# Block exchange on POOL's queue, later readers, the residual put away to DRAM, and probabilities of five head groups turned on VectorE and by DMA

## The chip, the core and the metric

The kernel runs on one core of a Trainium2 chip. The metric is the device time of one execution in microseconds, the median of several runs. TensorE (PE) multiplies, ScalarE (ACT) and VectorE (DVE) prepare and finish tiles, GpSimd (POOL) does small work and issues DMAs, SyncE (SP) issues DMAs.

## What is computed

Two transformer blocks on one sequence of 256 tokens of width 2048, in float32. The first has forget-gate ("fox") attention with 16 heads of 128 and a feed-forward part with a causal convolution of width 3; the second has 8 heads of dilated attention beside gated linear attention (GLA), and a SiLU-gated feed-forward part. Cut to the shape of the work:

```
h  = x
h += fox_attention(rms(h) @ w1) @ w2          # 16 heads, 4 groups of 4
h += (silu(conv(gate)) * conv(val)) @ w4      # gate, val = split(rms(h) @ w3), 2 x 5632 columns
q, k, v, ... = split(rms(h) @ w5)
h += concat(gla(...), dilated_attention(...)) @ w6   # 8 dilated heads, 2 groups of 4
h += (silu(rms(h) @ w7g) * (rms(h) @ w7u)) @ w8
```

The softmax of one head is `p = softmax(q k^T * scale + bias)`, causal, and its output `p v`.

## The kernel before

**Weights.** `plan` lists every weight tile, 128 x 2048, in order of use. `dma_to` loads them from SP's queue into three `raw` buffers. `split_to` turns half a tile at a time into a high part `wh` (a cast on ScalarE, line 105) and a low part `wl` (a subtraction on VectorE, line 111), five buffers of each. `gemm` walks over column blocks of 512 and, within one, over units: a unit is half a weight tile, and `mm3` (lines 118 to 120) makes twelve products of 128 x 512 of it. Before unit u is multiplied, the split of unit u + 4 is recorded (`LEAD = 4`), so ScalarE and VectorE may come up to four units late before TensorE stands still.

**Order.** Nothing reorders the program: every engine runs its instructions as they are recorded. All work beside the weight products is in generators. `gemm` calls `pump` after each unit but the last of a block, and `pump` takes one step of every generator in `fast` and of the first in `slow` (two steps of the latter while `rate[0]` is 2). After the last unit it starts the block's `evac` instead. A `yield` is therefore the distance of one unit, and a value is waited for by the engine whose next instruction reads it.

**Block exchange.** A block of 256 tokens x 512 columns has to be turned before it can be multiplied again. `flip` turns 32x32 pieces on VectorE (line 296), writes them in four DMAs, the legs, to a DRAM tile `way` (line 300) and reads it back in one, the return (line 304), all from SP's queue. Steps: transpose, one yield, legs, one yield, return, two yields, then the reader (`ordered`, line 316, four ScalarE operations that put the pieces in order into a new tile, or `split_flipped`). There are 54 flips, 216 legs.

**Attention.** For each group of four heads `plain` scales q and k, `head_norm` norms them (the square on ScalarE, the sum on VectorE, root and multiplication on POOL), `flip` turns them, and `box["kf"]` opens the generator `attention`: `s2` for scores and softmax (lines 429 to 448), `s3` for three TensorE transposes of the probabilities against the identity (line 456) and a copy from PSUM (line 459), `s4` for the product with v (lines 466 to 468). Each step does one head. In the fourth fox group q and k are turned on TensorE instead (`s1`, `flipped` is false). `fox_bias` makes the bias on POOL from `ckb`, the running sums of the gates, stored and broadcast to all partitions by POOL's queue in `fgate` (lines 601 and 605).

**Residual.** `h`, four blocks of 2 x 512, is loaded once and stays in SBUF, in four of the 33 slots that `alloc` hands out in turn; `resid` adds each column block of w2, w4 and w6 to it, and `out_evac` that of w8.

Of the kernel before, what the change touches and what calls it, by code (L numbers as in the profile page):

```python
# [43 lines left out]
def fox_gla_dilated_kernel(  # L44
# [94 lines left out]
    def dma_to(i):  # L139
        while next_dma[0] <= min(i, len(plan) - 1):  # L140
            k = next_dma[0]
            t = rawp.tile([P, 4, 512], F32, tag="raw", name="raw")
            src = plan[k].rearrange("p (k c) -> p k c", c=512)
            if k == 0:
                for q in range(4):
                    nc.sync.dma_start(out=t[:, q], in_=src[:, q])
            else:
                if k < KG:
                    load_x(k)
                if k < 3:  # L150
                    for q in (slice(0, 2), slice(2, 4)):
                        nc.sync.dma_start(out=t[:, q], in_=src[:, q])
                else:
                    nc.sync.dma_start(out=t, in_=src)
                if k == 3:
                    nc.sync.dma_start(out=cols[:, C_FFN:], in_=cols_d[:, C_FFN:])
                    nc.sync.dma_start(out=wn, in_=w_n.rearrange("p (a k c) -> p a k c", a=2, c=16))
                if k == 8:
                    nc.sync.dma_start(out=const, in_=const_d)
                if 4 <= k < 8:  # L160
                    c = k - 4
                    h[c] = alloc([2, 512], F32, f"h{c}")
                    nc.sync.dma_start(out=h[c], in_=x[:, c * 512:(c + 1) * 512].rearrange("(t p) c -> p t c", p=P))
            raw_t[k] = t
            next_dma[0] += 1
# [91 lines left out]
    h = {}  # L257
    xr = [alloc([4, S], F32, f"xr{i}") for i in range(KG)]
# [60 lines left out]
    def split_flipped(f, dst, gains):  # L319
# [7 lines left out]
        y = ordered(f, "y", gains)  # L327
# [4 lines left out]
        free(y)  # L332

    def resid(cb, ss, tt, gcol, rname, done):
        def evac(acc):
# [4 lines left out]
            if cb < KG - 1:  # L340
                sumsq(ss, cb, h[cb])
                f, held = yield from flip(h[cb])
                d = new_t(2, rname)
                split_flipped(f, d, gains)
                free(held)
                tt.extend(d)
                done.add(cb)
            else:
# [5 lines left out]
                sumsq(ss, cb, h[cb])  # L354
            if cb == KG - 1:
# [27 lines left out]
    def plain(name, box, key, r, norm=False, flipped=False, gain=None):  # L383
        def evac(acc):
# [12 lines left out]
            f, held = yield from flip(t_, t_)  # L397
            box[key + "f"] = ordered(f, name + "f", lambda kt: 1.0 if gain is None else gain)
            free(held)
        return evac  # L400

    def attention(box, gqk, bias_of, ot, done, tag, flipped, ready=None):
# [57 lines left out]

        def s4(i):
# [32 lines left out]
    def run_all():  # L494
# [43 lines left out]
        def x_rstd():  # L538
# [3 lines left out]
            for c in range(KG):  # L542
                sumsq(ss, c, h[c])
                yield
# [100 lines left out]
        for cb in range(4):  # L645
            gemm(ot, range(KG), resid(cb, ss, tt, C_FFN, "r2", d2), ready=lambda kg: kg in done1, last=cb == 3)
# [4 lines left out]
        def conv_evac(j, part, keep):  # L651
            cb = part * JF + j

            def evac(acc):
# [4 lines left out]
                f, held = yield from flip(u_, u_)  # L659
                n = ordered(f, "n")  # L660
                free(held)
                yield
                y = alloc([4, S], F32, "y")
                for kt in range(4):
                    ch = cb * 4 + kt
                    act.activation(out=y[:, kt], in_=n[:, kt], func=AF.Identity, scale=col(C_CW + 176 + ch),
                                   bias=col(C_CB + ch))
                for kt in range(4):
# [9 lines left out]
                if part == 0:  # L678
                    act.activation(out=y, in_=y, func=AF.Silu)
                    keep[j] = y  # L680
                    return
                sg = keep.pop(j)
                dve.tensor_tensor(out=y, in0=y, in1=sg, op=ALU.mult)
                free(sg)
# [6 lines left out]
                free(y)  # L691
# [11 lines left out]
        for cb in range(4):  # L703
            gemm(gt, range(JF), resid(cb, ss, tt, C_N1, "r3", d4), ready=lambda kg: 2 * kg + 1 in gt,
# [212 lines left out]
        for cb in range(4):  # L917
            gemm(mt, kgs6, resid(cb, ss, tt, C_N2, "r4", d6), ready=lambda kg: kg in d5, last=cb == 3)
# [14 lines left out]
        def up_evac(j):  # L933
            def evac(acc):
# [5 lines left out]
                f, held = yield from flip(t_, t_)  # L940
                d = new_t(2, "g")
                split_flipped(f, d, None)
                free(held)
# [20 lines left out]
        for cb in range(4):  # L964
            gemm(gt2, range(JF), out_evac(cb), ready=lambda kg: 2 * kg + 1 in gt2)
# [81 lines left out]
```

## Time and profile before

| | |
|---|---|
| median of 3 runs | 2262.06 us (2260.3 to 2266.52) |
| the profiled execution | 2266.26 us, its span 2264.5 us |
| busy share of the span | PE 99%, PEld 81%, DVE 56%, ACT 50%, POOL 5% |
| weight products | 784 units of 12 |
| DMA | 479.74 MB, 212 GB/s in the mean |

The span reaches from the first to the last instruction of the program; the rest of the execution's time lies around it. A busy time counts an engine's own instructions, not its waits. "Idle before, released by" names the instruction whose end the engine waited for. A line can be that of a helper: line 105 is any high part, line 111 any low part, line 316 any reordering after a flip.

### The profile page before, as it was taken

To read this page: it belongs to the slowest core of one execution; us is meant where nothing else is said; L and a number is where in the kernel's file an instruction comes from. 1 tells how busy PE (TensorE), PEld (TensorE's weight loads), DVE (VectorE), ACT (ScalarE), POOL (GpSimd) and SP (SyncE) were. 2 spreads that over 40 slices of the span, in tenths; PEclk is the share of its full clock that TensorE was granted. 3 is DMA by queue.
4 is the path that set the end of the run, shared out by engine and by line. 5 is a ranking of instruction groups with operands and counts; after the bars stand their busy time and mean duration, and the time that the engine had idled before them with its cause. 6 is when DMAs were issued, how large, how long until landed. Compare 5 with 4: busy or idle time off the path is not lost. (4 is left out here: it accounts for less than half of the span.)

```text
span 2264.5 us, 25811 instructions
## 1 busy us (share of the span) xinstructions
PE 2235.4 (99%) x9948; PEld 1829.2 (81%) x9948; DVE 1275.7 (56%) x1511; ACT 1141.7 (50%) x1565; POOL 115.6 (5%) x135
## 2 busy tenths in 40 slices
PE   9899999999999999999999999999999999999999
PEld 7778788888877777888887787788888888888887
DVE  5555556566666676645554654565555555554443
ACT  6555555556565656544455554554444444443332
POOL 1232120000000000000110200000000000000000
PEclk9999999999999999999999999999999999999999
DMA  7665547576767676666654564475665666665553
GB/s 297 238 205 189 183 167 242 204 249 215 243 221 240 225 236 229 234 212 207 239 193 161 205 200 172 151 240 205 224 221 206 219 227 207 220 223 206 203 199 117
DMA packets 101068, 479.74 MB, mean 212 GB/s; under 512 B 11312, under 2 KB 39872, under 8 KB 51152
## 3 DMA queue, kind: packets, MB, share of 16 engines
q1 hardware_dynamic: 99152, 474.23, 60.6%
q0 software_dynamic: 928, 3.20, 0.4%
q8 instruction: 78, 1.28, 0.2%
q10 hardware_dynamic: 864, 0.66, 0.1%
q14 instruction: 46, 0.38, 0.0%
HBM read 447.62 MB, written 30.43 MB: 211 GB/s over the span
## 5 line engine op out<-in xcount | busy, mean ns | idle before, releaser
L111 DVE TENSOR_TENSOR wl<-raw,wh 128x1024 fp32r<-128x1024 f32 (+1 forms) x786 | 956.4, 1227 | 821.8 <-ACT wh L105 821.5
L105 ACT CAST wh<-raw 128x1024 fp32r<-128x1024 f32 (+1 forms) x786 | 814.1, 1048 | 696.2 <-PE acc L120 661.5
L119 PE MATMUL acc<-wl,r 128*128 128x512 f32 x1792 | 702.0, 392 | 3.3 <-DVE wl L111 3.2
L118 PE MATMUL acc<-wh,r 128*128 128x512 f32 x1792 | 703.8, 393 | 0.0
L120 PE MATMUL acc<-wh,r 128*128 128x512 f32 x1792 | 698.5, 390 | 0.0
L119 PEld LDWEIGHTS acc<-wl,r 128*128 128x128 f32 x1792 | 337.0, 188 | 83.4 <-DVE wl L111 15.2
L118 PEld LDWEIGHTS acc<-wh,r 128*128 128x128 f32 x1792 | 337.0, 188 | 73.1 <-issue 2.5
L120 PEld LDWEIGHTS acc<-wh,r 128*128 128x128 f32 x1792 | 336.7, 188 | 69.7
L119 PE MATMUL acc<-wl,g 128*128 128x512 f32 x704 | 274.6, 390 | 0.6 <-DVE wl L111 0.6
L120 PE MATMUL acc<-wh,g 128*128 128x512 f32 x704 | 273.9, 389 | 0.0
L118 PE MATMUL acc<-wh,g 128*128 128x512 f32 x704 | 273.9, 389 | 0.0
L119 PEld LDWEIGHTS acc<-wl,g 128*128 128x128 f32 x704 | 132.1, 188 | 30.3 <-DVE wl L111 2.9
L118 PE MATMUL acc<-wh,x 128*128 128x512 f32 x384 | 155.7, 406 | 0.0
L118 PEld LDWEIGHTS acc<-wh,g 128*128 128x128 f32 x704 | 132.1, 188 | 27.6
L120 PEld LDWEIGHTS acc<-wh,g 128*128 128x128 f32 x704 | 132.1, 188 | 27.1
L119 PE MATMUL acc<-wl,x 128*128 128x512 f32 x384 | 150.1, 391 | 0.6 <-DVE wl L111 0.6
L120 PE MATMUL acc<-wh,x 128*128 128x512 f32 x384 | 150.2, 391 | 0.0
L316 ACT ACTIVATE n<-u 128x256 f32<-128x256 f32 x88 | 29.5, 406 | 136.2 <-DMA u<-way 136.2
L119 PEld LDWEIGHTS acc<-wl,x 128*128 128x128 f32 x384 | 72.5, 189 | 15.6 <-DVE wl L111 1.3
L120 PEld LDWEIGHTS acc<-wh,x 128*128 128x128 f32 x384 | 72.2, 188 | 15.7
L118 PEld LDWEIGHTS acc<-wh,x 128*128 128x128 f32 x384 | 72.5, 189 | 15.3 <-ACT wh L105 0.8
L671 DVE SCALAR_TENSOR_TENSOR y<-n,cols,y 128x255 f32<-128x255 f32 (+1 forms) x176 | 81.0, 481 | 3.1
(199 smaller groups left out, 1362.3 us busy)
## 6 DMA issues: line engine op xcount, KB each, us to landing
raw<-in_w_dram SPq DMA_DIRECT2D x301, 1024.0 KB, 4.9
raw<-in_w7g_dram SPq DMA_DIRECT2D x44, 1024.0 KB, 4.8
raw<-in_w7u_dram SPq DMA_DIRECT2D x44, 1024.0 KB, 5.0
way<-turn SPq DMA_DIRECT2D x216, 128.0 KB, 2.6
u<-way SPq DMA_DIRECT2D x22, 512.0 KB, 5.5
sg<-way SPq DMA_DIRECT2D x11, 512.0 KB, 4.8
flip<-way SPq DMA_DIRECT2D x9, 512.0 KB, 4.7
q<-way SPq DMA_DIRECT2D x6, 512.0 KB, 5.4
```

What stands on the lines that cost most here:

```text
L105: act.copy(out_, in_)
L111: dve.tensor_tensor(out=out_, in0=in_, in1=hi.bitcast(F32), op=ALU.subtract)
L118: pe.matmul(out_, xh, wh, start=first, stop=False)
L119: pe.matmul(out_, xh, wl, start=False, stop=False)
L120: pe.matmul(out_, xl, wh, start=False, stop=last)
L316: act.activation(out=grid(y[:, kt]), in_=f[:, kt], func=AF.Copy, scale=scale(kt))
L671: dve.scalar_tensor_tensor(out=yy[:, d:S], in0=n[:, kt, 0:S - d], scalar=col(C_CW + 176 - 88 * d + ch), in1=yy[:, d:S], op0=ALU.mult, op1= ...
```

## The change

Four things are edited.

1. `flip` issues legs and return from POOL's queue (`nc.gpsimd`), in a helper `exchange`, and yields four times after the return instead of twice. The tile of the transposes, `turn`, is kept and handed to the reader, which puts its ordered result there, so that no new tile is taken. In `plain` one more yield stands between `ordered` and the entry in `box`; in `conv_evac` the convolution's sum takes the place of the returned block, with one yield more before VectorE's part.
2. `fetch` loads a block of `h` just before its column block is multiplied, and `put_away` stores it to DRAM after `resid`; at the start SP loads the four blocks as before, and `x_rstd` frees each after use. `fetch` and `put_away` go through POOL's queue.
3. Where `flipped` is true, five of six groups, `s3` is replaced by `turned`: two heads at a time VectorE transposes the probabilities, `exchange` writes them to DRAM (192 of 256 columns wide), one return reads both heads, and three yields later ScalarE copies them into `pts`.
4. The order of steps follows: `s2` for four heads, `turned((0, 2))`, `s4`.

```
+    home = [x[:, c * 512:(c + 1) * 512].rearrange("(t p) c -> p t c", p=P) for c in range(KG)]
+
+    def fetch(c, queue=nc.gpsimd):
+        h[c] = alloc([2, 512], F32, f"h{c}")
+        queue.dma_start(out=h[c], in_=home[c])
+
+    def put_away(c):
+        home[c] = dramp.tile([P, 2, 512], F32, name=f"home{c}")
+        nc.gpsimd.dma_start(out=home[c], in_=h[c])
+        free(h.pop(c))
...
+    def exchange(turn, width):
+        way = ways.tile([P, 4, S], F32, tag="way", name="way")
+        for i in range(4):
+            nc.gpsimd.dma_start(out=way[:, i, 0:width].rearrange("(j c) e -> c j e", c=32),
+                              in_=turn[32 * i:32 * i + 32, :, 0:width])
+        return way[:, :, 0:width]
+
     def flip(src, into=None):
...
-        way = ways.tile([P, 4, S], F32, tag="way", name="way")
-        for i in range(4):
-            nc.sync.dma_start(out=way[:, i].rearrange("(j c) e -> c j e", c=32), in_=turn[32 * i:32 * i + 32])
+        way = exchange(turn, S)
         yield
         held = alloc([4, S], F32, "flip") if into is None else into
         f = held.rearrange("p a c -> p (a c)").rearrange("p (i e) -> p i e", i=4)
-        nc.sync.dma_start(out=f, in_=way)
-        yield
-        yield
-        free(turn)
-        return f.rearrange("p i (k t r) -> p k t i r", k=4, t=2), held
+        nc.gpsimd.dma_start(out=f, in_=way)
+        for _ in range(4):
+            yield
+        return f.rearrange("p i (k t r) -> p k t i r", k=4, t=2), held, turn
...
-    def ordered(f, name, scale=lambda kt: 1.0):
-        y = alloc([4, S], F32, name)
+    def ordered(f, y, scale=lambda kt: 1.0):
         for kt in range(4):
             act.activation(out=grid(y[:, kt]), in_=f[:, kt], func=AF.Copy, scale=scale(kt))
-        return y
...
@@ resid
+            put_away(cb)
             if cb == KG - 1:
                 rows[rname] = row_rstd(ss, rname)
...
@@ plain
-            f, held = yield from flip(t_, t_)
-            box[key + "f"] = ordered(f, name + "f", lambda kt: 1.0 if gain is None else gain)
+            f, held, y = yield from flip(t_, t_)
+            ordered(f, y, lambda kt: 1.0 if gain is None else gain)
             free(held)
+            yield
+            box[key + "f"] = y
...
@@ attention
+        def turned(pairs):
+            held = {}
+            for a in pairs:
+                turn = alloc([4, S], F32, "pturn")
+                for n in range(2):
+                    pb = sm.pop(a + n)
+                    dve.transpose(
+                        out=turn[:, :, n * 96:(n + 1) * 96].rearrange("p j (c r) -> p j c r", c=3),
+                        in_=pb[:, 0].rearrange("p (c j r) -> p j c r", c=3, j=4),
+                    )
+                    free(pb)
+                yield
+                way = exchange(turn, 192)
+                yield
+                held[a] = turn
+                nc.gpsimd.dma_start(out=turn[:, :, 0:192], in_=way)
+            for _ in range(3):
+                yield
+            for a in pairs:
+                f = held[a][:, :, 0:192].rearrange("p i (n c r) -> p n c i r", n=2, c=3)
+                for n in range(2):
+                    pt[a + n] = alloc([3, P], F32, "pts")
+                    act.copy(pt[a + n].rearrange("p c (i r) -> p c i r", i=4), f[:, n])
+                free(held[a])
+                yield
...
-        for s_ in ((s2, s3) if flipped else (s1, s2, s3)):
+        for s_ in ((s2,) if flipped else (s1, s2, s3)):
             while s_ is s2 and ready is not None and not ready():
                 yield
             for i in range(4):
                 s_(i)
                 yield
+        if flipped:
+            yield from turned((0, 2))
...
@@ before each column block of w2, w4, w6 and w8
+            fetch(cb)
```

Three places in the order of instructions show what moves. Line numbers in rows of the change are those of the changed file.

POOL in the first head group of the fox attention, before: k's multiplication, the store of the gates' sums, the four broadcasts `ckb`, and then the bias of the first head.

```order
L381 TENSOR_TENSOR k_544<-k_544,rsh_551 128x1024
L601 DMA cum_dram_611<-cumts_609 16x256
L605 DMA ckb0_613<-cum_dram_611 128x1024
L605 DMA ckb1_615<-cum_dram_611 128x1024
L605 DMA ckb2_617<-cum_dram_611 128x1024
L605 DMA ckb3_619<-cum_dram_611 128x1024
L614 TENSOR_SCALAR pb_727<-ckb0_613,cum_146 128x128
```

The same place in the change (`way` and `turn` are the tiles of an exchange).

```order
L392 TENSOR_TENSOR k_544<-k_544,rsh_551 128x1024
L303 DMA way_596<-turn_577 32x4x256 x4
L643 DMA cum_dram_611<-cumts_609 16x256
L647 DMA ckb0_613<-cum_dram_611 128x1024
L647 DMA ckb1_615<-cum_dram_611 128x1024
L647 DMA ckb2_617<-cum_dram_611 128x1024
L647 DMA ckb3_619<-cum_dram_611 128x1024
L318 DMA q_470<-way_596 128x1024
L303 DMA way_659<-turn_640 32x4x256 x4
L318 DMA k_544<-way_659 128x1024
L656 TENSOR_SCALAR pb_798<-ckb0_613,cum_146 128x128
```

q's legs now stand ahead of the store and the broadcasts, q's return and k's exchange behind them.

POOL in the second head group of the change, from q's multiplication to k's; before, no DMA stood between these two.

```order
L392 TENSOR_TENSOR q_965<-q_965,rsh_972 128x1024
L303 DMA way_996<-pturn_946 32x4x192 x4
L489 DMA pturn_946<-way_996 128x4x192
L303 DMA way_1042<-pturn_1018 32x4x192 x4
L303 DMA way_1063<-turn_1039 32x4x256 x4
L489 DMA pturn_1018<-way_1042 128x4x192
L318 DMA q_965<-way_1063 128x1024
L241 TENSOR_SCALAR rsh_1149<-hms_1147 128x8
L242 TENSOR_TENSOR rsh_1149<-rsh_1149,mhalf_82 128x8
L392 TENSOR_TENSOR k_1142<-k_1142,rsh_1149 128x1024
```

Two exchanges of the first group's probabilities (`pturn`) have come in, around q's exchange.

ScalarE in the first group of the second attention, from k's scaling to the ordered k, before.

```order
L389 ACTIVATE k<-acc_8898,rsr_8766 128x512
L389 ACTIVATE k<-acc_8899,rsr_8766 128x512
L375 ACTIVATE sq<-k 128x1024
L105 CAST wh<-raw 128x1024 x7
L316 ACTIVATE kf<-k 128x256 x4
```

The same in the change.

```order
L400 ACTIVATE k<-acc_8880,rsr_8748 128x512
L400 ACTIVATE k<-acc_8881,rsr_8748 128x512
L386 ACTIVATE sq<-k 128x1024
L105 CAST wh<-raw 128x1024 x2
L328 ACTIVATE turn<-q,gqk 128x256 x4
L105 CAST wh<-raw 128x1024 x6
L400 ACTIVATE v<-acc_9040,rsr_8748 128x512
L400 ACTIVATE v<-acc_9041,rsr_8748 128x512
L105 CAST wnarrow<-wn 128x16x16
L105 CAST wh<-raw 128x1024 x2
L328 ACTIVATE turn<-k 128x256 x4
```

Ten casts of a unit's weights stand ahead of the ordered k instead of seven, and the reading of q comes in between.

## Rows read from the trace of the kernel before

**Rows 1.** The page's part 1: busy us, share of the span, instructions.

```profile
PE 2235.4 (99%) x9948; PEld 1829.2 (81%) x9948; DVE 1275.7 (56%) x1511; ACT 1141.7 (50%) x1565; POOL 115.6 (5%) x135
```

**Rows 2.** Waits of TensorE: engine, line, waited for; us in total, times, longest.

```profile
PE sc L429 <- ACT kf L316: 19.1, 5, 6.5
PE acc L119 <- DVE wl L111: 4.5, 9, 0.8
```

**Rows 3.** TensorE's timeline: start, us, operation, in brackets the wait before it.

```profile
83.87 0.80 PE L429 MATMUL sc<-kf,qf 128*128 128x128 f32 x2 [6.49 <-ACT kf L316]
...
160.24 0.49 PE L429 MATMUL sc<-kf,qf 128*128 128x128 f32 x2 [2.26 <-ACT kf L316]
...
1206.65 0.80 PE L429 MATMUL sc<-kf,qf 128*128 128x128 f32 x2 [3.85 <-ACT kf L316]
...
1292.09 0.80 PE L429 MATMUL sc<-kf,qf 128*128 128x128 f32 x2 [4.17 <-ACT kf L316]
```

**Rows 4.** The same after two scores; one row of busy times by stretch (PEclk after POOL).

```profile
1210.10 0.39 PE L120 MATMUL acc<-wh,r 128*128 128x512 f32 x1
...
1206.00:1210.00 4.00, 3.35 (x9) 2.79 (x10) 0.80 (x5) 3.79 (x10) 0.00 (x0) 0.57 0.07 31
...
1299.84 0.38 PE L429 MATMUL sc<-kf,qf 128*128 128x128 f32 x2
...
1301.64 0.40 PE L120 MATMUL acc<-wh,r 128*128 128x512 f32 x1
```

**Rows 5.** TensorE's timeline around two sets of transposed probabilities.

```profile
1310.05 0.49 PE L456 MATMUL pt<-const,pb 128*128 128x128 f32 x3
...
1310.61 0.40 PE L119 MATMUL acc<-wl,r 128*128 128x512 f32 x1
...
1312.91 0.39 PE L120 MATMUL acc<-wh,r 128*128 128x512 f32 x1
1313.14 0.49 PE L456 MATMUL pt<-const,pb 128*128 128x128 f32 x3
```

**Rows 6.** Timelines of VectorE, SP's queue and ScalarE: k's exchange ahead of 1206.65.

```profile
1194.40 1.31 DVE L296 STREAM_TRANSPOSE turn<-k 128x512 f32<-128x512 f32 x2 [2.36 <-POOL k L381]
...
1195.74 1.77 SPq L300 DMA_DIRECT2D way<-turn  x4
...
1200.06 0.34 SPq L304 DMA_DIRECT2D k<-way  x1
...
1206.18 1.33 ACT L316 ACTIVATE kf<-k 128x256 f32<-128x256 f32 x4 [5.01 <-DMA k<-way]
```

**Rows 7.** DMA issues: tiles, queue, count, KB each, median us from issue to landing.

```profile
way<-turn SPq DMA_DIRECT2D x216, 128.0 KB, 2.6
...
k<-way SPq DMA_DIRECT2D x6, 512.0 KB, 5.3
...
ckb<-cum_dram POOLq DMA_DIRECT2D x4, 512.0 KB, 10.9
...
rel<-in_rel_dram POOLq DMA_DIRECT2D x2, 512.0 KB, 5.2
...
cum_dram<-cumts POOLq DMA_DIRECT2D x1, 16.0 KB, 5.4
```

**Rows 8.** POOL's timeline in the first head group.

```profile
67.43 0.73 POOL L601 DMA_DIRECT2D cum_dram<-cumts  x1
73.11 2.16 POOL L605 DMA_DIRECT2D ckb<-cum_dram  x4 [4.94 <-DMA cum_dram<-cumts]
80.70 0.38 POOL L614 TENSOR_SCALAR pb<-ckb,cum 128x128 f32<-128x128 f32 x1 [5.43 <-DMA ckb<-cum_dram]
```

**Rows 9.** The instructions of tile `ckb`: landing of its four transfers.

```profile
DMA to landing us min/median/max: 7.5/10.9/13.4
```

**Rows 10.** Waits of ScalarE for the returned blocks of the conv stage.

```profile
ACT n L316 <- DMA u<-way: 136.2, 22, 7.8
```

**Rows 11.** The page's part 3: DMA queue of SP: packets, MB, share.

```profile
q1 hardware_dynamic: 99152, 474.23, 60.6%
```

More of the change, by code (lines that the diff above doesn't have):

```diff
@@ L160, in dma_to @@
                 if 4 <= k < 8:
-                    c = k - 4
-                    h[c] = alloc([2, 512], F32, f"h{c}")
-                    nc.sync.dma_start(out=h[c], in_=x[:, c * 512:(c + 1) * 512].rearrange("(t p) c -> p t c", p=P))
+                    fetch(k - 4, nc.sync)
             raw_t[k] = t
@@ L326, in split_flipped @@
             return
-        y = ordered(f, "y", gains)
+        ordered(f, y, gains)
         for half in range(2):
@@ L331, in split_flipped @@
             lo_of(d[:, :, 1], y[:, sl], d[:, :, 0])
-        free(y)
     def resid(cb, ss, tt, gcol, rname, done):
@@ L341, in evac @@
                 sumsq(ss, cb, h[cb])
-                f, held = yield from flip(h[cb])
+                f, held, turn = yield from flip(h[cb])
                 d = new_t(2, rname)
-                split_flipped(f, d, gains)
-                free(held)
+                split_flipped(f, turn, d, gains)
+                free(held, turn)
                 tt.extend(d)
@@ L543, in x_rstd @@
                 sumsq(ss, c, h[c])
+                free(h.pop(c))
                 yield
@@ L658, in evac @@
                 yield
-                f, held = yield from flip(u_, u_)
-                n = ordered(f, "n")
-                free(held)
+                f, held, n = yield from flip(u_, u_)
+                y = held.rearrange("p a c -> p (a c)").rearrange("p (k s) -> p k s", k=4)
+                ordered(f, n)
                 yield
-                y = alloc([4, S], F32, "y")
                 for kt in range(4):
@@ L667, in evac @@
                                    bias=col(C_CB + ch))
+                yield
                 for kt in range(4):
@@ L679, in evac @@
                     act.activation(out=y, in_=y, func=AF.Silu)
-                    keep[j] = y
+                    keep[j] = (y, held)
                     return
-                sg = keep.pop(j)
+                sg, spent = keep.pop(j)
                 dve.tensor_tensor(out=y, in0=y, in1=sg, op=ALU.mult)
-                free(sg)
+                free(spent)
                 yield
@@ L690, in evac @@
                     lo_of(d[:, :, 1], y[:, sl], d[:, :, 0])
-                free(y)
+                free(held)
             return evac
@@ L703, in run_all @@
         for cb in range(4):
+            fetch(cb)
             gemm(gt, range(JF), resid(cb, ss, tt, C_N1, "r3", d4), ready=lambda kg: 2 * kg + 1 in gt,
@@ L917, in run_all @@
         for cb in range(4):
+            fetch(cb)
             gemm(mt, kgs6, resid(cb, ss, tt, C_N2, "r4", d6), ready=lambda kg: kg in d5, last=cb == 3)
@@ L939, in evac @@
                 yield
-                f, held = yield from flip(t_, t_)
+                f, held, turn = yield from flip(t_, t_)
                 d = new_t(2, "g")
-                split_flipped(f, d, None)
-                free(held)
+                split_flipped(f, turn, d, None)
+                free(held, turn)
                 gt2[2 * j], gt2[2 * j + 1] = d
@@ L964, in run_all @@
         for cb in range(4):
+            fetch(cb)
             gemm(gt2, range(JF), out_evac(cb), ready=lambda kg: 2 * kg + 1 in gt2)
```

2 lines of the change are left out of this document (1 added, 1 removed).

## The prediction

> **What bounds the kernel now.** Part 1 of the page comes first: the reader is to see that TensorE is busy for 2235.4 of 2264.5 us [rows 1], so that only work that TensorE drops, or time in which it stands still, can move the end. Next come the waits: five waits for `kf` (line 429 behind line 316) hold 19.1 us and nine waits for `wl` hold 4.5 us, 23.6 of the 29.1 us in which TensorE is idle [rows 2]. The timeline of TensorE then shows four of the five: 6.49 us in the first head group, 2.26 in the next (the third is alike), 3.85 and 4.17 in the two groups of the second attention [rows 3]. VectorE (56%), ScalarE (50%) and POOL (5%) have room; what counts there is when a result arrives, not how busy they are.
>
> The clock adds to the long waits. After 3.85 us without work the granted clock was 0.57 of full from 1206 to 1210 us, most of it spent at the lower level (1.2 GHz). The score products and five weight products that follow took 3.45 us (1206.65 to 1210.10), and the same ones without a wait 1.80 us (1299.84 to 1301.64), so such a wait costs 1.6 us more [rows 3, 4]. The waits of 6.49 and 4.17 us show the same 0.80 us form of the first products; the 2.26 us wait shows 0.49, near the undisturbed 0.38, and I give it nothing.
>
> **The change, part by part.**
> *Transposes on TensorE.* Line 456's three products leave in five of six groups: 5 x 4 heads = 20 sets. From one set to the next, with twelve weight products between, TensorE took 3.09 us (1310.05 to 1313.14); ten weight products took 2.30 us (1310.61 to 1312.91), so twelve 2.76, and a set costs 0.33 us [rows 5]. All of it is on the path: 20 x 0.33 = **6.6 us less**. In its place VectorE gets 20 transposes of 128x384. Two of 128x512 took 1.31 us [rows 6], hence about 0.5 us each, 10 us in all, beside a VectorE that is 44% idle; I cost them at nothing. If that cover went, `wl` would be late, which is the wait of 4.5 us above. ScalarE keeps its 20 copies, from SBUF now.
>
> *Later readers.* A unit (twelve weight products, 2.76 us) lies between two steps of a generator. A block exchange is now read six units after VectorE's transpose, not four, and in the attentions the first score stands four units later: 27 units, not 23, stand ahead of it in TensorE's order, and likewise in the other groups. This gives k's chain 4 x 2.76 = 11.0 us more.
>
> *Exchange on POOL's queue.* On SP the four legs out and the return were issued at 1195.74 and 1200.06, 4.3 us apart, and the return landed in 5.3 us [rows 6, 7], 9.6 together. POOL issues a leg in 0.54 us (2.16 for four) [rows 8]. What a leg takes to land from POOL no row shows; near it stand a 16 KB store to DRAM, 5.4 us, and 512 KB loads, 5.2 us, against 2.6 us for an SP leg of 128 KB [rows 7]. With the store for the last leg and the load for the return the exchange takes 3 x 0.54 + 5.4 + 5.2 = 12.2 us, **2.6 us later than on SP**. From below it is -0.1 (a leg of 2.6 as on SP and a return of 5.3), from above 13.8 (10.9 us per leg, the median of four 512 KB broadcasts queued together). I take 2.6, since the store is of the same kind. The Trainium skill's page "DMA: Bandwidth & Descriptors" (Specifications) gives a first byte after about 1 us on GpSimd's path against 0.6 us on SP's; by that alone two legs would be an estimated 0.8 us later, the 1 us put on late probabilities below would go, and the sum would be -18.8 us. The rows speak for more: 16 KB from POOL took twice as long as 128 KB from SP [rows 7].
>
> *Four of the five waits.* 11.0 - 2.6 = 8.4 us is more than 4.17, so the waits in all groups but the first go: 19.1 - 6.5 = 12.6 us, and twice 1.6 us of clock: **15.8 us less**. Next late would be the turned probabilities: their second return stands on POOL behind q's legs, and ScalarE may stand a unit or so for it, against four units of split weights that lie ready. In the third group, where generators step twice per unit, the output products follow at once; I put 1 us (0 to 3) on that.
>
> *The first group.* Here POOL's queue is the cost. At 67.43 us POOL was free and stored the sums, 5.7 us later (73.11) it began the four `ckb` broadcasts, and the last landed 13.4 us after its issue [rows 8, 9]. Now q's four legs go first (2.2 us: the store starts at 69.6, the broadcasts at 75.3). The last broadcast was issued at 74.7 and landed at 88.1, 15.0 after the first issue, now 90.3. q's return and k's legs stand behind it: three broadcasts landed between 80.7 and 88.1, 2.5 us each, so q's return lands at 92.8, k's legs at 95.3, k's return is issued by 95.8, lands at 101.1, and ScalarE's first of four copies (1.33 us together [rows 6]) ends at 101.5. TensorE reached the wait at 77.4 (83.87 - 6.49) and now reaches it at 88.4: it waits 13.1 us instead of 6.49, **6.6 us more**. From below: if k's legs pass the broadcasts, landing in 5.4 us after 80.2, the return goes out at 86.1 and the wait is 3.4 us, 3.1 less than before. From above: a leg and a return at 13.4 us each, after 80.2, give 107.9 and a wait of 19.5, 13.0 more. I take the queue in order, as the broadcasts' own landings grew from 7.5 to 13.4 us.
>
> *The conv stage.* ScalarE waited 136.2 us in 22 flips for `u`, 6.2 each, 7.8 at most [rows 10]. Two units more and the exchange 2.6 us longer make it 6.2 - 5.5 + 2.6 = 3.3. TensorE's waits for `wl` fall in stretches where ScalarE came late, so most of 4.5 us should go: **3 us less** (0 to 4.5).
>
> *The rest at nothing.* The residual goes to DRAM 12 times and comes back 16 times: 28 x 512 KB, with ten exchanges of probabilities 22 MB more on the 474 of SP's queue, which fills 60.6% of the DMA engines [rows 11]; a block is fetched a whole column block ahead of its use. Work that covers it: 8 or more units of products; without that cover each fetch would cost its landing, 5.2 us [rows 7]. POOL gets some 350 issues at 0.54, 190 us of a nearly idle engine, and SP loses 270, which had nothing late behind them.
>
> Sum: -6.6 - 15.8 - 3 + 6.6 + 1 = **-17.8 us**. The profiled execution had a span of 2264.5 us and a time of 2266.26; it becomes 2248.5. The median of the runs is 4.2 us below that execution, so I forecast **2244.3 us**. With the bounds (first group -3.1 to +13.0, conv 4.5 to 0, late probabilities 0 to 3) the gain is 30.0 to 6.4 us: 2232 to 2256.
>
> **The rivals.** *The waits move, no change.* ScalarE takes its instructions in order, and its reads of the turned probabilities and of q now stand ahead of k's squares or of the scores' exponentials. If each comes 3 to 6 us late, k's chain starts late by as much and the four waits return at their old size: -6.6 - 3 + 6.6 + 1 = -2.0 us, 2260 us. For it speaks POOL's order in the second group, two exchanges of probabilities ahead of q's return and of k's norm; against it, the 8.4 us to spare and the four units of split weights. Chance 0.11.
>
> *POOL's legs are slow, slower.* If one leg takes longer than about 7.8 us the flips come later than the readers everywhere. At 9.2 us per leg (between the 7.5 of the first broadcast and the 10.9 median [rows 9]) the exchange is 3 x 0.54 + 18.4 - 9.6 = 10.4 us later. In the conv stage ScalarE then waits 6.2 - 5.5 + 10.4 = 11.1 us, 3.3 beyond the 7.8 that TensorE rode out, 22 times: 73 us. The first group loses another 7.8, and of the four waits 10.2 of 12.6 us stay, with the clock's share: +73 + 6.6 + 7.8 + 1 - 6.6 - 2.4 = +79, 2341 us. It decides at 7.8 us: there the delay is 7.6, each flip overruns by 0.5 us (11 us), the first group loses 11.6, and the gains of 22.4 are used up. Against it: single transfers from POOL took 5.2 and 5.4 us, and no issue row shows starvation, 0.54 to 0.73 us [rows 7, 8]. The Trainium skill's "SBUF — State Buffer" (SBUF: two separate sides) has a rule on this side: descriptors of GpSimd's DMAs can't be written while VectorE runs an operation in a two-port mode; an estimate by its 620 against 3100 ns, over the five issues of an exchange, is some 12 us later, which would be this rival. No row here bears it out. Chance 0.09.
>
> *It doesn't do what it says* has no room for the transposes, since they are not in TensorE's order any more; for the waits it is the first rival.
>
> **How the numbers follow.** Forecast 0.80, first rival 0.11, second 0.09. A measurement of this kernel can tell 0.3% (6.8 us) from no change. The forecast's cases lie nearly all over 6.8 us of gain, so faster 0.79; no change takes the first rival and a rest of the forecast, 0.12; slower 0.09. The range is the forecast's own, carried a little toward the first rival: 2233 to 2258.
>
> **What would show it.** Right: 12 products of `pt` instead of 72, waits for the scores only in the first group, and longer there, near 13 us; ScalarE's wait for `u` near 3 us; legs from POOL landing in about 5 us. Wrong: waits at scores of later groups, waits of TensorE for `wl` throughout the conv stage, or POOL's legs over 7.8 us.

## The result, and the profile after

The changed kernel takes 2245.59 us (2238.77 to 2248.14, four runs) against 2261.67 us before; the ratio is 0.9922 with a 95% interval of 0.9899 to 0.9946. The forecast was 2244.3. The profiled execution took 2246.22 us, its span 2244.4. A gain of 16 us was forecast at 17.8, but the terms behind it were not all right, and the ledger shows it. It is worked out from the starts of the weight products in the traces: the start of a unit's first product after, less its start before, and from that the difference over each stretch. The last column does the same for the first experiment, which is told below. It compares one execution of each kernel, and the one before lies 4.6 us over its median; so about 4 of its 20.1 us belong to that execution and not to the change, and it does not say in which stretch.

```
stretch (units)                        forecast   after    exchange on SyncE
start (0 to 22)                           0        +2.0       +1.3
first head group (22 to 30)              +6.6      -2.1       -9.5
rest of the fox attention (30 to 102)    -7.5      -8.0       -8.4
w2 to its end (102 to 130)                0       +10.3       +0.2
w3, convolution (130 to 307)             -3.0     -13.3      -13.3
w4, start of w5 (307 to 414)              0        -1.0       -1.0
second attention (414 to 470)           -13.9     -14.5      -14.5
w6 to its end (470 to 522)                0        +6.6       +0.1
rest                                      0        -0.1       -0.1
sum                                     -17.8     -20.1      -45.2
```

The attentions came out as forecast. Three stretches did not: the convolution gave 10 us more, the first group 9 us more, and the ends of w2 and w6, to which the sum gave nothing, took 17 us. These errors cancel, and that they do is luck. The 2.0 us at the start belong to no edit that the runs below could find: all twelve pass that place sooner, by 0.2 to 1.9 us.

First the waits of TensorE (engine, line, waited for; us in total, times, longest), after the change:

```profile
PE tp L290 <- DVE h L347: 12.2, 3, 7.6
PE sc L442 <- ACT turn L328: 5.6, 1, 5.6
PE acc L118 <- ACT wh L105: 1.2, 1, 1.2
PE acc L119 <- DVE wl L111: 0.8, 1, 0.8
```

Against [rows 2], four of the five waits for scores are gone, and so are eight of nine waits for `wl`. The top line is new: before the transposes of the residual's last block TensorE waits for VectorE's sum of that block. The timeline of TensorE (start, us, operation, in brackets the wait before it) puts the places at the first scores and at the ends of w2 and w6:

```profile
95.82 0.80 PE L442 MATMUL sc<-turn 128*128 128x128 f32 x2 [5.55 <-ACT turn L328]
...
408.44 2.35 PE L290 MATMUL tp<-const,h 128*128 128x128 f32 x8 [7.55 <-DVE h L347]
...
1522.15 0.35 PE L290 MATMUL tp<-const,h 128*128 128x128 f32 x1 [4.37 <-DVE h L347]
```

What leads to 408.44 is one block's chain in w2, from its sum to the next block's sum, in the timelines of VectorE, POOL and ScalarE:

```profile
382.99 1.28 DVE L347 TENSOR_TENSOR h<-acc,h 128x512 f32<-128x512 f32 x2
385.32 1.30 DVE L312 STREAM_TRANSPOSE turn<-h 128x512 f32<-128x512 f32 x2
405.09 1.29 DVE L111 TENSOR_TENSOR r<-turn,r 128x512 fp32r<-128x512 f32 x2 [6.22 <-ACT r L105]
407.69 1.28 DVE L347 TENSOR_TENSOR h<-acc,h 128x512 f32<-128x512 f32 x2
...
386.91 2.24 POOL L303 DMA_DIRECT2D way<-turn  x4 [14.02 <-DVE turn L312]
397.42 0.56 POOL L318 DMA_DIRECT2D flip<-way  x1 [8.28 <-DMA way<-turn]
...
402.84 1.70 ACT L328 ACTIVATE turn<-flip,cols 128x256 f32<-128x256 f32 x4 [5.24 <-DMA flip<-way]
```

Sum, turn, legs (10.5 us from the first to the return's issue), return (5.4), reader, and behind the reader on VectorE the next block's sum: 24.7 us from sum to sum, while eight units of 2.72 us take TensorE 21.8. Each block of w2 is later than the one before, and the last is waited for. In the convolution a block has eight units too, but nothing there hangs the next block's first step on this block's reader.

In the convolution TensorE's products in a stretch (PE's busy us come second, in brackets the products begun) tell more than its waits, first before, then after:

```profile
640.00:700.00 60.00, 58.49 (x252) 46.47 (x251) 35.70 (x48) 33.54 (x52) 0.00 (x0) 1.00 0.66 231
```

```profile
640.00:700.00 60.00, 60.00 (x266) 49.71 (x265) 40.99 (x52) 38.03 (x55) 8.27 (x15) 1.00 0.73 243
```

Before, TensorE was busy for 58.49 of 60 us, 2.5% short, and yet began 252 products where it now begins 266, 5% fewer. A busy time beside a late split is longer than the work in it; by this ledger the 4.5 us of listed waits [rows 2] were a third of what the late splits cost. How much of that the later readers took away is the subject of experiments 4 and 5.

### The profile page after: what moved, and what is told of

Read it like the earlier page. It is cut to its first block, busy times and chain, and to the rows that moved or that the text cites. A ratio compares the mean times of both kernels' runs of the same rounds, so it can differ in the third digit from the quotient of the medians.

```text
span 2244.4 us, 25865 instructions
## 1 busy us (share of the span) xinstructions
PE 2219.1 (99%) x9888; PEld 1827.7 (81%) x9888; DVE 1290.0 (57%) x1531; ACT 1148.9 (51%) x1565; POOL 316.3 (14%) x483
## 4 chain that ended last, share of the span: by engine, by line
PE 91%; DMA 4%; ACT 1%; POOL 1%; DVE 1%; issue 1%; ACTq 0%; DVEq 0%; POOLq 0%; SPq 0%
PE acc L118 29%; PE acc L120 29%; PE acc L119 29%; DMA way<-turn 2%; DMA flip<-way 1%; POOL way L303 1%; ACT wh L105 1%; PE sc L443 0%; DMA xr<-in_x_t_dram 0%; DMA way<-pturn 0%; ACT turn L328 0%; PE nar L603 0%; DMA ckb<-cum_dram 0%; DVE h L347 0%; PE sc L442 0%
## 5 line engine op out<-in xcount | busy, mean ns | idle before, releaser
L303 POOL DMA_DIRECT2D way<-turn x216 | 119.5, 560 | 984.0 <-DVE turn L312 909.0
L714 DVE SCALAR_TENSOR_TENSOR u<-turn,cols,u 128x255 f32<-128x255 f32 (+1 forms) x176 | 80.9, 481 | 3.1
```

The costliest lines, as they stand in the source:

```text
L303: nc.gpsimd.dma_start(out=way[:, i, 0:width].rearrange("(j c) e -> c j e", c=32), in_=turn[32 * i:32 * i + 32, :, 0:width])
L714: dve.scalar_tensor_tensor(out=yy[:, d:S], in0=n[:, kt, 0:S - d], scalar=col(C_CW + 176 - 88 * d + ch), in1=yy[:, d:S], op0=ALU.mult, op1= ...
```

## The experiments

Each differs from the changed kernel, or from the experiment that is named, by what its diff shows. Line numbers in an experiment's rows are those of its own file.

**1. Exchange on SyncE.**

```diff
-            nc.gpsimd.dma_start(out=way[:, i, 0:width]...
+            nc.sync.dma_start(out=way[:, i, 0:width]...
-        nc.gpsimd.dma_start(out=f, in_=way)
+        nc.sync.dma_start(out=f, in_=way)
-                nc.gpsimd.dma_start(out=turn[:, :, 0:192], in_=way)
+                nc.sync.dma_start(out=turn[:, :, 0:192], in_=way)
```

> The change with all legs and returns issued by SyncE again; later readers, turned probabilities and the residual's trips stay. Theory A (loop): at the ends of w2 and w6 TensorE stood 7.55 and 4.37 us before the transposes of h, because one block's chain (sum, turn, legs, return, reader, next block's sum behind that reader on VectorE) takes 24.7 us there with POOL's exchange, more than the 22 us in which TensorE goes through eight units, so that lateness adds up over three blocks. On SyncE the legs take 4.3 us to the return's issue where POOL took 8.6 to 10.5; the chain becomes about 20 us, both waits go, and with the low clock behind them about 17 us; the first head group's 5.6 us for the scores goes too (nothing stands behind the broadcasts). Time near 2222 us. Rival B (order): it is the reader's later place, ahead of the last block's sum, that makes the waits; they stay at 4 us or more each and the time is near 2238. Rival C: legs that wait for VectorE on SyncE hold up the weight loads now that everything comes later; waits for the split weights appear in the convolution and the time is 2245 or more.

Measured: 2221.12 us (2220.41 to 2221.36), ratio to before 0.9813 (0.9791 to 0.9836). These are the only waits of TensorE that remain:

```profile
PE warm L571 <- DVE warm L568: 1.4, 1, 1.4
PE acc L119 <- DVE wl L111: 0.8, 1, 0.8
PE acc L118 <- ACT wh L105: 0.7, 1, 0.7
```

B and C fall: the readers stand where they stood, and the convolution keeps its 13.3 us. From sum to sum the blocks of w2 now take 22.6, 21.8 and 21.7 us, so that lateness no longer adds up. This is the best version of this study. SyncE's timeline shows one exchange in it:

```profile
416.53 1.78 SPq L303 DMA_DIRECT2D way<-turn  x4
418.41 0.39 SPq L154 DMA_DIRECT2D raw<-in_w_dram  x1
420.80 0.34 SPq L318 DMA_DIRECT2D u<-way  x1
```

The return is issued 4.3 us after the first leg, as before the change; the median is 4.4 in the convolution, and 6.5 in the residual's nine flips.

**2. Residual's readers two units earlier.**

```diff
-    def flip(src, into=None):
+    def flip(src, into=None, wait=4):
...
-        for _ in range(4):
+        for _ in range(wait):
...
-                f, held, turn = yield from flip(h[cb])
+                f, held, turn = yield from flip(h[cb], wait=2)
```

> The change with two yields instead of four between return and reader in the residual's flips of w2, w4 and w6 alone. Theory A (loop): the reader still ends when its data have landed, and the next sum still stands behind it, so both waits for the transposes of h stay (within 2 us of 7.55 and 4.37); time 2245. Rival B (order): with the reader two units further from the last sum both waits go, about 17 us less, 2229.

Measured: 2252.53 us (2250.78 to 2258.57).

```profile
PE tp L290 <- DVE h L347: 11.2, 3, 6.3
```

The waits stay, so the reader's place was not their cause: 5.0 us at the end of w2 and 6.3 at that of w6, where the change has 7.6 and 4.6. The time is 7 us over what A gave; TensorE besides runs out of splits (`wh` and `wl` 5.0 us together, 2.0 in the change).

**3. Residual's readers two units later.** The same edit with `wait=6`.

> The change with six yields between return and reader in the residual's flips alone, so that the next block's sum stands ahead of the reader on VectorE and the chain no longer closes on itself. Theory A (loop): no lateness adds up; the waits before the transposes of h at the ends of w2 and w6 fall to under 1 us, though the first products of the next stage that need the third block may wait up to 3 us; time 2229 to 2234. Rival B (order: later is worse): the waits grow by two units, 5 us each; 2255.

Measured: 2229.57 us (2228.12 to 2231.63). No wait for the transposes of h is left; the next sum now stands ahead of the reader on VectorE, and lateness no longer adds up:

```profile
396.28 1.28 DVE L347 TENSOR_TENSOR h<-acc,h 128x512 f32<-128x512 f32 x2
...
402.71 1.30 DVE L111 TENSOR_TENSOR r<-turn,r 128x512 fp32r<-128x512 f32 x2 [0.91 <-ACT r L105]
```

Runs 1, 2 and 3 together show the loop: a quicker exchange opens it, an earlier reader does not, a reader behind the next sum does.

**4. Convolution's readers two units earlier.** `flip(u_, u_, wait=2)` in `conv_evac` alone.

> The change with two yields instead of four between return and reader in the convolution's 22 flips alone. From unit 130 to unit 330 the change gained some 14 us on the kernel before, where I had put 3. Theory A (later readers made it): ScalarE now waits 22.8 us in 22 flips, 1 us each; two units less give 1 + 5.5 = 6.5 us each, about as before, and the gain of 14 us goes: 2259. Rival (the exchange on POOL, off SyncE's queue, freed the weight loads): units stay at 2.72 us and the time at 2245.

Measured: 2361.09 us (2354.85 to 2363.25), ratio 1.0426 (1.0393 to 1.0459). The direction was expected, the size was not: 115 us more than the change, where 14 were expected (in the ledger 110.8 of them lie in the stretch of w3). ScalarE's waits for the returned block after the change, and then, in this run, TensorE's waits and ScalarE's:

```profile
ACT turn L328 <- DMA u<-way: 22.8, 22, 2.0
```

```profile
PE acc L118 <- ACT wh L105: 55.5, 21, 3.7
PE acc L119 <- DVE wl L111: 16.3, 22, 0.8
...
ACT turn L328 <- DMA u<-way: 209.4, 22, 11.3
```

At 1.0 us per flip TensorE loses nothing; at 5.7 (experiment 5) it loses 6.4 us in 22 flips against the change, 0.3 each; at 6.2 (before [rows 10]) it lost 13.3, 0.6 each; at 9.5 it loses 110.8, 5.0 each. From these points I estimate that four units of split weights, which take TensorE 10.9 us, cover about 6 us of ScalarE's absence. Beyond that the whole delay is on the path and more: from 6.2 to 9.5 us, 3.3 us of wait cost 4.4, and the granted clock was 0.93 to 0.95 in this stretch (500 to 900 us), where it was 1.00 before (640 to 880). So the later readers are what POOL's queue needed: without them in the convolution alone the change would have been 4% slower. Why they took 8.5 us per flip off ScalarE's wait and not the 5.5 of two units is not settled; ScalarE no longer works off a backlog ahead of each reader, which would bring it there later, but no run separates that.

**5. SyncE, with the readers as early as before.** On experiment 1:

```diff
-        for _ in range(4):
+        for _ in range(2):
...
             free(held)
-            yield
             box[key + "f"] = y
...
                                bias=col(C_CB + ch))
-                yield
```

> The exchange on SyncE as in the first experiment, and besides the later readers taken back (two yields after the return, none more in the attentions and the convolution), so that of the change only the turned probabilities and the residual's trips are left. Theory: the later readers are what removed the waits for the scores and the late units of the convolution; both come back (some 13 us in the convolution, 13 to 16 in the four later head groups, 7 to 8 in the first) and the time is the kernel before less the transposes, 2255. Rival (taking the residual out of SBUF or turning the probabilities on VectorE relieved something else): the time stays under 2240.

Measured: 2255.38 us (2252.94 to 2259.11), ratio 0.9972 (0.9958 to 0.9985).

```profile
PE sc L441 <- ACT turn L328: 15.3, 4, 6.6
...
ACT turn L328 <- DMA u<-way: 124.6, 22, 7.8
```

The waits for the scores and for `u` are back. The later readers are worth 34 us on SyncE's queue (2255.38 to 2221.12); turned probabilities and put-away residual alone leave the kernel 7 us under the 2262.48 of the kernel before, measured beside it, about the 6.6 us of the transposes.

One stretch did not go back as expected. In the ledger w3 stands 6.9 us under the kernel before although its readers stand as early (13.3 less 6.4), and from 640 to 700 us TensorE begins 265 products, not 252. So the readers are shown to be worth 6.4 of the 13.3 us on this queue. The other 6.9 may be a difference between executions (the two profiled ones lie 5.4 us further apart than the medians) or come from another edit; no run separates these.

**6. and 7. Probabilities on TensorE again**, on SyncE's queue and on POOL's:

```diff
-        for s_ in ((s2,) if flipped else (s1, s2, s3)):
+        for s_ in ((s2, s3) if flipped else (s1, s2, s3)):
...
-        if flipped:
-            yield from turned((0, 2))
```

> The exchange on SyncE with later readers, the probabilities of all groups transposed on TensorE as before. Theory: 20 sets of 0.33 us come back, all on the path: 2221.1 + 6.6 less up to 1 us of lateness in the third group, 2227. Rival (the sets cost nothing where TensorE waits anyway, or the turned probabilities have a late cost of the same size): 2221 to 2223.

> The change with the probabilities of all groups transposed on TensorE as before, everything else kept, the exchange on POOL. Theory: 6.6 us come back less the 1 us of lateness: 2251. Rival (the ten exchanges of probabilities crowd POOL's queue, and k's exchange behind them comes late): 2246 or less.

Measured: 2228.58 us (2228.15 to 2230.55), 7.5 more than experiment 1, and 2250.33 (2246.73 to 2252.78), 4.7 more than the change, where the ranges touch. The 20 sets are on the path at 0.33 us each [rows 5]. The two differences are 2.8 us apart, within the spread of the change's own runs. The ledger is finer: in the two stretches of the attentions the sets cost 7.4 us on SyncE's queue and 7.1 on POOL's, so at most 0.3 us of lateness shows, and TensorE waited 0.2 us in all for copied probabilities in the change.

**8. and 9. The first head group**, both on experiment 3. The sums' store and the broadcasts go to SyncE:

```diff
-            pool.dma_start(out=sc, in_=cs[0:16])
+            nc.sync.dma_start(out=sc, in_=cs[0:16])
...
-                pool.dma_start(out=ckb[g], in_=sc...
+                nc.sync.dma_start(out=ckb[g], in_=sc...
```

> The version with six yields in the residual's flips, POOL still issuing the exchange, with the store of the gates' sums and the four broadcasts moved to SyncE's queue, so that nothing but q's and k's exchange stands on POOL in the first head group. Theory (queue): k's reader waited for what stood behind 2 MB of broadcasts; TensorE's wait of about 5 us for the first scores falls under 1 us and with the low clock after it the time goes from 2229.6 to about 2222. Rival: POOL's own slow legs make that wait, q's exchange then k's, each 13 us; it falls by less than 2 us, 2228.

The second leaves them on POOL and sends three of them later:

```diff
             for g in range(4):
+                if g:
+                    for _ in range(8):
+                        yield
                 ckb[g] = alloc(...)
...
-                                  lambda: ckb[3] is not None))
+                                  lambda g=g: ckb[g] is not None))
```

> Six yields in the residual's flips, POOL issuing the exchange; of the four broadcasts of the gates' sums only the first group's is sent where it was, the others eight units apart behind it. Theory (bytes: 2 MB of broadcasts run on the same DMA engines while k's legs are under way, from whichever queue they are sent): k's legs come back to the 8.6 us that they take elsewhere, from 11 to 14, TensorE's wait of 4.7 us for the first scores falls to 2 us or less and the time from 2229.6 to about 2225. Rival (POOL's exchange of q and then k is too slow by itself): the wait stays over 4 us, 2229.

Measured: 2229.90 us (2228.47 to 2231.60), nothing gained, and 2227.47 (2222.78 to 2236.22), which is not told apart from 2229.57. POOL's timeline of the first of the two:

```profile
67.53 2.42 POOL L303 DMA_DIRECT2D way<-turn  x4
77.19 0.57 POOL L318 DMA_DIRECT2D q<-way  x1 [7.25 <-DMA way<-turn]
77.76 2.19 POOL L303 DMA_DIRECT2D way<-turn  x4
89.02 0.56 POOL L318 DMA_DIRECT2D k<-way  x1 [9.07 <-DMA way<-turn]
```

k's legs still need 11.3 us to the return's issue with nothing else on POOL's queue, and TensorE waits 4.94 us, so the place of the broadcasts in that queue was not the cause. With the broadcasts spread, TensorE's first wait did fall, but a second one came (first experiment 3, then the two waits of this run):

```profile
94.20 0.80 PE L442 MATMUL sc<-turn 128*128 128x128 f32 x2 [4.73 <-ACT turn L328]
...
91.72 0.80 PE L442 MATMUL sc<-turn 128*128 128x128 f32 x2 [2.49 <-ACT turn L328]
...
167.93 0.80 PE L442 MATMUL sc<-turn 128*128 128x128 f32 x2 [3.70 <-ACT turn L328]
```

It fell from 4.73 to 2.49 us in the first group. In the second, where experiment 3 has no wait, a broadcast now stands between k's legs and k's return, which lands in 7.6 us and not in 4.8, and TensorE waits 3.70. The theory's 8.6 us for k's legs did not come: they took 11.4 us to the return's issue, against 13.0 in experiment 3. That is 1.6 us less; about as much was won because POOL no longer issues three broadcasts (0.54 us each) ahead of k's legs. So the broadcasts' bytes are a part of the first wait, and how the rest divides, between two exchanges on POOL one behind the other and other transfers, stays open.

**10. Half the weights of w3.** `dma_to` loads `t[:, 0:2]` alone for the tiles 64 to 151 and `split_to` uses that half twice: the second half of each weight tile of w3 is left out.

> The change with the second half of every weight tile of w3 not loaded: its first half is used in its place, so each of these loads is 512 KB and not 1 MB, and all else is the same. Theory (POOL's legs stand behind the weight load: in the convolution the packets of the first leg run about 1.1 us after its issue, then those of the weight load issued 2 to 3 us after the legs take the DMA engines for some 4 us, then the legs' rest): POOL's wait from the last leg to the return falls from 6.7 us to about 4.5. Rival (POOL's own path, its descriptors or its writing of them beside VectorE, is what is slow): it stays over 6 us.

What it is about stands in the DMA queues of the change, in three pieces of one exchange of the convolution (legs issued from 500.64 us, return at 509.39): 500.6 to 503.5, 503.5 to 506.5, and 506.5 to 509 (queue: packets, MB, share of 16 engines; q0 is POOL's, q1 SyncE's):

```profile
q0 software_dynamic: 97, 0.30, 54.3%
q1 hardware_dynamic: 13, 0.02, 2.2%
...
q1 hardware_dynamic: 96, 0.79, 78.7%
q0 software_dynamic: 47, 0.09, 9.4%
...
q1 hardware_dynamic: 53, 0.30, 38.1%
q0 software_dynamic: 48, 0.13, 13.1%
```

The legs' first 0.30 MB go at once; then a weight load comes in (issued 1.4 us after the first leg, not 2 to 3), and for 3 us the legs get 0.09 MB beside its 0.79; the rest goes when the load is nearly done. Measured with half loads (one time, 2237.85 us), POOL's timeline of the same kind of exchange:

```profile
491.06 2.19 POOL L306 DMA_DIRECT2D way<-turn  x4 [13.95 <-DVE turn L315]
498.60 0.57 POOL L321 DMA_DIRECT2D u<-way  x1 [5.36 <-ACT u L725]
```

7.5 us to the return's issue where the change took 8.75 (500.64 to 509.39); over the 22 exchanges of the convolution the median falls from 9.0 to 7.4, and POOL's wait per return from 6.7 us to 5.2, where 4.5 was expected. That is most of the fall expected, so the load's share is shown; what is left between 7.4 and SyncE's 4.4 may be the other half of the load or POOL's own path, and that stays open.

**11. and 12. The residual's trips**, doubled on POOL, and moved to SyncE:

```diff
-        queue.dma_start(out=h[c], in_=home[c])
+        for _ in range(2 if queue is nc.gpsimd else 1):
+            queue.dma_start(out=h[c], in_=home[c])
...
-        nc.gpsimd.dma_start(out=home[c], in_=h[c])
+        for _ in range(2):
+            nc.gpsimd.dma_start(out=home[c], in_=h[c])
```

> The change with every load and store of the residual on POOL's queue issued twice (28 more transfers of 512 KB, 14.7 MB). Theory (the residual's trips are hidden and no cause of the waits): the same waits of TensorE, the time within 3 us of the change's 2245.6. Rival (the trips lengthen POOL's exchange in w2 and w6, where store and load stand behind each return): the waits before the transposes of h grow by 2 us or more each, with the low clock 2251 or more.

```diff
-    def fetch(c, queue=nc.gpsimd):
+    def fetch(c, queue=nc.sync):
...
-        nc.gpsimd.dma_start(out=home[c], in_=h[c])
+        nc.sync.dma_start(out=home[c], in_=h[c])
```

> The change with the residual's loads and stores issued by SyncE, in line with the weight loads, the exchange still on POOL. Theory (POOL's queue: store and load stand right behind each return and run beside it and the next legs; in the run with doubled trips the waits grew by 5.5 us): the returns of w2 and w6 land in about 5 us, not 6 to 7, and TensorE's waits before the transposes of h fall from 12.2 us to 8 or less, 2239 to 2241. Rival (the same bytes use the same DMA engines, and the weight loads come later behind them): the waits stay within 2 us of 12.2 or grow, 2244 or more.

Measured: 2252.51 us (2250.13 to 2253.73) and 2238.80 (2230.63 to 2243.28). Waits of TensorE, doubled and moved:

```profile
PE tp L292 <- DVE h L349: 17.7, 2, 9.3
```

```profile
PE tp L290 <- DVE h L347: 7.2, 3, 6.4
```

And the DMA issues of w2 (330 to 412 us; KB each, median us to landing), in the change and with the trips on SyncE:

```profile
home<-h POOLq DMA_DIRECT2D x4, 512.0 KB, 6.4
flip<-way POOLq DMA_DIRECT2D x3, 512.0 KB, 6.1
```

```profile
home<-h SPq DMA_DIRECT2D x4, 512.0 KB, 8.7
flip<-way POOLq DMA_DIRECT2D x3, 512.0 KB, 4.7
```

In w2 the trips are not free where they stand. The store is issued right behind the return and runs beside it; off POOL's queue the return lands in 4.7 us, not 6.1, and of the 7.6 us of wait at the end of w2 0.8 are left (6.0 in experiment 7, where the trips are the change's). In w6 this is not shown: there the return landed in 6.2 us after 6.4, and the wait grew from 4.6 to 6.4 us. The time fell by 6.8 us, and its range overlaps that of the change. The doubled run is less clean, since there the second store of a pair waits for the first and holds POOL up.

## Why the prediction was right, and where not

*Transposes.* Right: 6.6 us forecast, 7.1 to 7.5 on SyncE's queue (experiments 5 and 6).

*Later readers and the four waits.* Right: all four went, and both attention stretches came within 0.6 us of their forecast. The 1 us for late probabilities was too much (experiments 6 and 7).

*The exchange on POOL.* The step "2.6 us later than on SP" was too small. Legs to return took 9.0 us at the median of the convolution, the return 5.0, together 14.0 against 9.6: 4.4 later. I had taken the single 16 KB store's 5.4 us for the last leg, and a leg beside a weight load takes longer (experiment 10). The sign that I had named, legs landing in about 5 us, was met (4.7 at the median of 216) and said little: from the last leg's issue to the return's it was some 7 us. The estimate by the Trainium skill's "DMA: Bandwidth & Descriptors" (Specifications), 0.8 us later, was further off. The first packets of these exchanges did run 1.1 to 1.2 us after the issue, about the 1 us of that page of the Trainium skill; an exchange waits for its last ones.

*The first group.* The step "k's legs behind the broadcasts" had the order right and the sizes too large. POOL and ScalarE after the change:

```profile
71.87 0.52 POOL L643 DMA_DIRECT2D cum_dram<-cumts  x1
74.84 2.15 POOL L647 DMA_DIRECT2D ckb<-cum_dram  x4 [2.45 <-DMA cum_dram<-cumts]
76.98 0.53 POOL L318 DMA_DIRECT2D q<-way  x1
...
91.57 0.56 POOL L318 DMA_DIRECT2D k<-way  x1 [9.43 <-DMA way<-turn]
...
89.77 1.70 ACT L328 ACTIVATE turn<-q,gqk 128x256 f32<-128x256 f32 x4 [12.01 <-DMA q<-way]
```

The sums' store landed in 2.7 us, not the 5.4 of [rows 7], and k's return was issued at 91.6, not 95.8. With the start 2.0 us later, the return's issue lies 6.2 us ahead of the forecast and the scores 7.6, and TensorE, which came to the wait at 90.3 us, stood for 5.55 us and not for 13.1. On SyncE q and k are exchanged ahead of the broadcasts and the wait is gone.

*The convolution.* The step that failed is the price of late splits, "most of 4.5 us": in the ledger the listed waits stood for 13.3 us of later products, of which experiment 5 shows 6.4 to be the readers'. ScalarE's wait for `u`, forecast at 3.3 us a flip, came to 1.0 although the exchange was 4.4 us later and not 2.6; why is the open point of experiment 4. The 7.8 us that I took as what TensorE rides out was wrong as well; the cover is about 6 us.

*The rest at nothing.* This failed at w2 and w6, by 16.9 us. I priced the slower exchange in the attentions and the convolution and not in the residual's flips, where a block has eight units and the next block's sum stands behind this block's reader; and I asked whether a fetch comes in time, not what a store does to the return beside it, which counted in w2.

*The rivals.* "The waits move" came true in part and elsewhere: the scores' waits went, and 16.9 us of 37 came back at the ends of w2 and w6. "POOL's legs are slow" did not decide, but only because of the readers' two units: experiment 4, without these in the convolution, shows what it describes, 9.5 us of wait per flip and 2361 us. Its rule from the Trainium skill's "SBUF — State Buffer" (SBUF: two separate sides) did not show itself: by the timelines of POOL and VectorE, legs to return take 8.5 us at the median in the feed-forward part of the second block, where VectorE is busy for some 47% of that time, and 9.0 in the convolution, where it is busy for 86%; and half loads shortened it to 7.4 with VectorE's work unchanged. Whether any of VectorE's operations there runs in a two-port mode no run shows, so the rule itself is not tested.

So the time was met within 1.3 us by luck, with a right account of the attentions and the transposes and with three other terms wrong: the first group 8.7 and the convolution 10.3 us too dear, the ends of w2 and w6 16.9 us too cheap.

## What to carry to other kernels

A longer latency costs nothing, or all of itself and more, by how many units of prepared work lie ahead of the engine that waits for it: look for each loop in which the next round's first step stands behind this round's last, and compare its length with the round's work. Read a stretch's loss from the products begun per microsecond against an undisturbed stretch, not from the listed waits. And when a latency is to be hidden by reading later, keep the quick queue as well: on SyncE's queue this change is worth 41 us, on POOL's 16.

## What the runs showed of the hardware that I had not expected

A queue of its own does not make a transfer independent. Legs on POOL's queue shared the 16 DMA engines with the 1 MB weight load issued 1.4 us after the first of them and got 0.09 MB in 3 us beside its 0.79; on SyncE's queue the same load stood behind the legs, and in the convolution the return was issued after 4.4 us at the median rather than 9.0.

POOL's transfers signal eight semaphores in turn, so a ninth waits for the first: in the first group the fourth of k's legs was issued only when the first broadcast, eight issues ahead of it, had landed.

```profile
77.50 1.68 POOL L303 DMA_DIRECT2D way<-turn  x3
81.59 0.55 POOL L303 DMA_DIRECT2D way<-turn  x1 [2.41 <-DMA ckb<-cum_dram]
```

The clock again charged for long waits: after 7.55 us without work the granted clock of the next 4 us was 0.50 of full, the lower of the two levels (1.2 GHz), and eight transposes took 2.35 us (1.03 in the kernel before, without the wait).

```profile
408.40:412.40 4.00, 3.84 (x13) 3.17 (x14) 3.07 (x5) 1.31 (x3) 0.54 (x1) 0.50 0.80 285
```
